# A two-layer block with three token mixers on one core: another order of the projection's chunks, and the preparation of one branch beside the chain of another

## The chip, the cores and the metric

The kernel runs on one core of one Trainium2 chip. The metric is the device time of one execution in microseconds. The engines are called PE (TensorE), DVE (VectorE), ACT (ScalarE), POOL (GpSimd) and SP (SyncE, which here only issues transfers). Each engine works through its own instructions in the order in which they stand in its queue, and semaphores order the engines among each other.

## What is computed

512 tokens of width 1024 pass a first block (attention with pooling, then a mixture of experts) and a second block of two layers. Only the second block's two layers are touched. One such layer, cut to what matters:

```python
h = rms_norm_2(x, norm_g[layer])
cols = split_columns(h @ w_in[layer])          # gate, gdn q/k/v/a/b, mla cq/ckv/kr, rwkv r/k/v/wd/ad
y_gdn = gdn_branch(cols, ...)                  # depthwise conv, silu, gated delta rule, both directions
y_mla = mla_branch(cols, ...)                  # 6 heads of softmax attention over low-rank q and kv
y_rwkv = rwkv7_branch(cols, ...)               # 4 heads, recurrence with its own decay, both directions
mix = jnp.concatenate([y_gdn, y_mla, y_rwkv], axis=-1) * jax.nn.silu(cols['gate'])
x = x + mix @ w_out[layer]

# gdn_branch, per chunk of 64 tokens and head (gated_delta_chunked)
a_mat = beta[..., :, None] * jnp.einsum('nhcid,nhcjd->nhcij', k, k) * d_strict
sol = lax.linalg.triangular_solve(a_mat, rhs, left_side=True, lower=True, unit_diagonal=True)
p_intra = jnp.einsum('nhcid,nhcjd->nhcij', q, k) * d_incl
def step(s, inp):                              # over the 8 chunks
    u = u0_c - jnp.einsum('nhcd,nhde->nhce', w_c, s)
    o = jnp.einsum('nhcd,nhde->nhce', qg_c, s) + jnp.einsum('nhij,nhje->nhie', p_c, u)
    s = ge_c[..., None, None] * s + jnp.einsum('nhcd,nhce->nhde', kd_c, u)
    return s, o
```

## The kernel before

**The projection.** `Project` multiplies the normalized tokens by `w_in` in 27 chunks of 128 output columns. A chunk is 24 matmuls of 128x512 (`columns`, L1221: eight slices of the width, each as the three products hh·wh, hl·wh, hh·wl of a split into two parts). `load` (L1201) fetches a chunk's weights `w` by SP into a ring of two buffers ("pjw"); ACT rounds them to `wh` (L1212), and `wl = w - wh` (L1214) is made by DVE and POOL in turn, two chunks ahead. A ring buffer is free once `wl` is made. The chunk's sum lands in one of three PSUM buffers named "mm". The order before (`self.plan`, L1140 to L1142): first the small columns, then k (three chunks), q (three), v (three), gate 0 to 3, rw 0 to 6, ckv, cq, gate 4 to 7.

**What follows a chunk.** `qkv` (L1276) convolves and activates a chunk on ACT and DVE (four DVE operations on L1289, three more steps to L1299) into `y`, and puts the "take" of the chunk on a list; the take runs when three are pending. `take_q` sums squares on PE (`ssq`). `take_k` transposes to `kt`. `take_v` transposes eight tiles through the single PSUM buffer "tr" and copies each group to `VS` with two operations (L1444), one on ACT and one on DVE. `rw` (L1310) evicts a chunk of the RWKV7 columns with one operation of ACT and two of DVE (L1318, L1319).

**The gated delta branch** (`Gdn`). `keys` (L1500) normalizes `kt` on DVE (L1515), transposes it on PE into `kq`. `squares` (L1549) multiplies k by k for each of four token tiles t (PE, PSUM tile "x2"), ACT copies to `KK`, and DVE multiplies four quarters of 32 partitions into `M` (L1565; 16 operations of 32x384 in a layer). `decays` (L1567) builds `DT` and multiplies it by k·q: 8 DVE operations that read PSUM (L1601), two for each t. `inverse` (L1606) writes `M` to memory and reads it back transposed (`mud`, `au`: L1609, L1612), solves all blocks by 60 DVE operations (`solve`, L1342 and L1344), writes the inverse out and back (`xud`, `XT`: L1618, L1620), transposes on DVE (L1631, L1633), and joins the blocks by 96 small matmuls `x<-XT,AO` and 96 `x<-LT,XT`. `chain` (L1644) then runs eight steps: matmuls `kp`, DVE (L1660, L1662), matmuls `pu`, DVE (L1671), matmuls `kp`, DVE (L1684). An output phase of four rounds follows (L1716, L1729).

**The other branches.** `Rwkv.prepare` (L1802) has per direction a part `scaled` (`lw` L1832, then `BB`, `KR`, `s`, `sq` on L1844 to L1874, with POOL and ACT between), then a triangular solve of its own and `mm<-XT,AO`. `states` (L2021) is its recurrence. `mla` (L2147) is attention in 24 score units (`mm<-kT,qT`, `e`, `mo`), and `Mix` (L2277) gates, transposes (`tr<-mix`) and multiplies by `w_out`.

**What sets the order.** PE's order is written by the program: `weave` and `braid` run several generators ("streams") in turn, and a stream's `yield n` keeps it away for n us of planned PE time. The queues of the other engines are ordered by a scheduler with priorities. In `second` (L2394) the streams were woven so: (1) `first` (gates, triangles, keys, squares, then inverse beside decays) with `project`; (2) `second` (the chain) with `project`; (3) the rest of `project`; (4) `prepare` with `others` (mla, then two thirds of Mix) until prepare ends; (5) `states` with `others`.

## Time and profile before

| | us |
|---|---|
| median of 3 runs | 1932.96 |
| lowest and highest | 1924.71, 1935.54 |
| profiled execution | 1931.57 |
| its span (first to last instruction) | 1929.8 |
| granted clock of PE, mean, as a share of full speed | 0.912 |

The profile is of one execution. Its times count from the start of the span; 1.8 us lie around the span. The second block's first layer stands at about 834 to 1383, the second at about 1383 to 1922. Three kinds of view are used: the waits of an engine (what it waited for, in total, how many times, the longest), the timeline of an engine (each row a run of like instructions, with start and length), and busy times of all engines in a stretch with the granted clock.

### The profile page before, as it was taken

The numbers are of one execution on the slowest core, as the hardware profiler recorded it, in microseconds if no ns is written. First come the engines' busy times: TensorE is split into PE (matmuls) and PEld (weight loads), VectorE is DVE, ScalarE is ACT, GpSimd is POOL, SyncE is SP. The second block draws the span as 40 slices with busy tenths as digits, with TensorE's granted clock in tenths as the row PEclk, the third lists the DMA queues.
The fourth block names the chain that finished last, engine by engine and source line by source line (L and its number), as shares of the span: only waits on it lengthen the run. The fifth ranks groups of instructions, "written<-read, shape, count | busy, mean of one in ns | idle before, by whom it ended". The sixth has DMA issues, their size and how long they took to land.

```text
span 1929.8 us, 34104 instructions
## 1 busy us (share of the span) xinstructions
PE 1675.8 (87%) x14010; PEld 1119.3 (58%) x14010; DVE 1062.8 (55%) x2260; ACT 573.9 (30%) x1134; POOL 548.8 (28%) x559
## 2 busy tenths in 40 slices
PE   5999998999999999968788978768896899888777
PEld 3986584454544444447576746545675677556455
DVE  2435534353434343357796476745867875667437
ACT  3345432212122121154322125331343231154312
POOL 1113111101010101045641154254354612544443
PEclk7899998999999999979898988888898899797888
DMA  9924626999999999532243120143422341301332
GB/s 308 243 94 151 245 66 250 392 393 394 407 402 397 395 406 398 211 112 77 55 148 73 57 75 2 43 138 99 120 74 70 106 110 63 80 1 28 106 118 80
DMA packets 243218, 337.10 MB, mean 175 GB/s; under 512 B 92768, under 2 KB 166160, under 8 KB 226224
## 3 DMA queue, kind: packets, MB, share of 16 engines
q1 hardware_dynamic: 241152, 329.88, 49.6%
q10 hardware_dynamic: 1152, 3.22, 0.5%
q8 instruction: 112, 1.84, 0.4%
q0 software_dynamic: 752, 1.76, 0.3%
q14 instruction: 50, 0.41, 0.1%
HBM read 310.84 MB, written 23.99 MB: 174 GB/s over the span
## 4 chain that ended last, share of the span: by engine, by line
PE 26%; DVE 16%; issue 5%; DMA 4%; POOL 3%; ACT 2%; SPq 0%; DVEq 0%; POOLq 0%; ACTq 0%
PE mm L149 18%; DVE au L1344 2%; PE mm L159 2%; DVE stmp L1342 2%; PE x L149 2%; PE tr L149 1%; PE pu L149 1%; PE kp L149 1%; DVE M L1565 1%; POOL w L2308 1%; DMA w<-in_w_out_dram 1%; DVE wl L1214 1%; PE tr L159 1%; DVE y L1289 1%; PE mo L149 1%
## 5 line engine op out<-in xcount | busy, mean ns | idle before, releaser
L149 PE MATMUL gu<-w,XT 128*64 128x512 f32 x1024 | 225.8, 594 | 0.0
L149 PE MATMUL mm<-hh,wh 128*128 128x512 f32 (+1 forms) x464 | 202.1, 436 | 1.9 <-DVE rw L1319 1.9
L149 PE MATMUL mm<-hl,wh 128*128 128x512 f32 (+1 forms) x464 | 187.3, 404 | 0.0
L149 PE MATMUL mm<-hh,wl 128*128 128x512 f32 (+1 forms) x464 | 187.2, 403 | 0.0
L928 POOL TENSOR_TENSOR yl<-y,yh 128x512 fp32r<-128x512 f32 x30 | 38.1, 1271 | 451.3 <-ACT yh L927 451.3
L149 PEld LDWEIGHTS gu<-w,XT 128*64 128x64 f32 x1024 | 72.1, 137 | 142.7 <-issue 135.6
L938 DVE TENSOR_TENSOR xres<-mm,xres 128x512 f32<-128x512 f32 x128 | 79.2, 681 | 90.6 <-PE mm L149 90.6
L1212 ACT ACTIVATE wh<-w 128x1024 fp32r<-128x1024 f32 (+1 forms) x54 | 57.0, 1055 | 192.8 <-PE mm L149 134.1
L149 PE MATMUL mm<-w,hT 128*64 128x512 f32 x512 | 113.4, 595 | 0.7 <-ACT hT L912 0.7
L149 PEld LDWEIGHTS mm<-hh,wh 128*128 128x128 f32 (+1 forms) x464 | 91.3, 197 | 27.9 <-issue 5.7
L149 PEld LDWEIGHTS mm<-hh,wl 128*128 128x128 f32 (+1 forms) x464 | 90.6, 195 | 21.0
L2236 POOL TENSOR_SCALAR e<-e,rs 128x512 f32<-128x512 f32 x48 | 79.1, 1651 | 80.0 <-DVE rs L2235 58.1
L149 PEld LDWEIGHTS mm<-hl,wh 128*128 128x128 f32 (+1 forms) x464 | 91.6, 197 | 17.5 <-DVE hl L1160 0.2
L1214 POOL TENSOR_TENSOR wl<-w,wh 128x1024 fp32r<-128x1024 f32 (+1 forms) x28 | 68.1, 2431 | 112.3 <-ACT wh L1212 101.7
L149 PE MATMUL mm<-wh,hh 128*128 128x256 f32 x320 | 94.0, 294 | 2.2 <-ACT hh L357 2.2
L149 PE MATMUL mm<-wh,hl 128*128 128x256 f32 x320 | 91.2, 285 | 4.2 <-DVE hl L359 4.0
L149 PE MATMUL mm<-w,mh 128*128 128x512 f32 x256 | 88.6, 429 | 6.7 <-ACT mh L2359 4.1
L149 PE MATMUL mm<-wl,hh 128*128 128x256 f32 x320 | 90.7, 284 | 1.6 <-DVE wl L381 1.6
L149 PEld LDWEIGHTS mm<-w,hT 128*64 128x64 f32 x512 | 35.3, 137 | 66.7 <-issue 61.7
L1342 DVE TENSOR_TENSOR stmp<-au 96x60 f32<-96x60 f32 (+29 forms) x120 | 60.2, 501 | 16.0 <-DMA au<-rmud 8.7
L872 ACT ACTIVATE X<-mm,ws 128x512 f32<-128x512 f32 x32 | 22.0, 689 | 151.9 <-DVE ws L869 128.7
L926 DVE SCALAR_TENSOR_TENSOR y<-mm,ws,g2b 128x512 f32<-128x512 f32 x32 | 24.0, 751 | 78.2 <-PE mm L149 78.2
(580 smaller groups left out, 3678.4 us busy)
## 6 DMA issues: line engine op xcount, KB each, us to landing
w<-in_w_gate_dram SPq DMA_DIRECT2D x64, 1024.0 KB, 13.0
w<-in_w_up_dram SPq DMA_DIRECT2D x64, 1024.0 KB, 13.0
w<-in_w_down_dram SPq DMA_DIRECT2D x64, 1024.0 KB, 9.8
w<-in_w_in_dram SPq DMA_DIRECT2D x52, 512.0 KB, 4.1
w<-in_w_ada_dram SPq DMA_DIRECT2D x24, 1024.0 KB, 8.4
w<-in_w_out_dram SPq DMA_DIRECT2D x16, 512.0 KB, 4.1
w<-in_w_in_dram SPq DMA_DIRECT2D x6, 1024.0 KB, 11.9
w<-in_w_out_dram SPq DMA_DIRECT2D x4, 1024.0 KB, 6.3
```

What stands on the lines that cost most here:

```text
L149: return self.nc.tensor.matmul(out, a, b, **kw)
L159: return self.nc.tensor.transpose(out, a, ident)
L872: nc.scalar.activation(X[:, 512 * i:512 * i + 512], ps, AF.Copy, scale=ws[:, 1:2])
L926: nc.vector.scalar_tensor_tensor(y, py, ws[:, 0:1], net.g2b[:, hs], op0=ALU.mult, op1=ALU.mult)
L928: (nc.vector if last else nc.gpsimd).tensor_tensor(yl[:, hs], y, yh[:, hs].bitcast(F32), op=ALU.subtract)
L938: nc.vector.tensor_tensor(net.xres[:, t, hs], po, net.xres[:, t, hs], op=ALU.add)
L1212: nc.scalar.activation(h[:, :, :m], w[:, :, :m], AF.Copy)
L1214: eng.tensor_tensor(lo[:, :, :m], w[:, :, :m], h[:, :, :m].bitcast(F32), op=ALU.subtract)
L1289: nc.vector.scalar_tensor_tensor(y[:, lo:hi], ps[:, lo + d:hi + d], cw[:, j, m:m + 1], y[:, lo:hi], op0=ALU.mult, op1=ALU.add)
L1342: nc.vector.tensor_tensor(tv, au[:n, :, j + 1:, j:j + 1].to_broadcast(sh), au[:n, :, j:j + 1, 0:j].to_broadcast(sh), op=ALU.mult)
L1344: nc.vector.tensor_tensor(au[:n, :, j + 1:, 0:j], au[:n, :, j + 1:, 0:j], tv, op=ALU.add)
L2236: nc.gpsimd.tensor_scalar(e, e, rs, None, op0=ALU.mult)
```

## The change

The order of the chunks becomes: small columns, k (three), gate 0 to 3, q, v, rw, and the rest as before. The takes are no longer run by `qkv` but by `columns`, when two more chunks have been multiplied after the chunk they belong to. `keys` waits for 19 us of planned PE time rather than 14 before it normalizes. `take_v` copies by ACT only. `M` is multiplied for two token tiles at once: eight DVE operations of 32x768 in a layer rather than 16 of 32x384. The product k·q is copied out of PSUM by ACT into a tile `kr`, and one DVE operation of 128x768 per token tile multiplies it into `DT`. `prepare` is no longer a stream of its own: it runs at the end of `project`, so it is woven with the chain, and `others` begins only when the last chunk is done and the projection's buffers are released.

```diff
--- before.py
+++ after.py
@@ -1138,9 +1138,11 @@
         self.psum = ctx.enter_context(pool(tc, "pjp", 1, "right", PSUM))
         one = lambda n, i, w=128: [(OFF[n] + 128 * i, w)]
         self.plan = [FIRST]
-        self.plan += [one("qkv", m) for m in QKV]
-        self.plan += [one("gate", m) for m in range(4)] + [one("rw", m) for m in range(7)] + [one("ckv", 0), one("cq", 0)] + [one("gate", m) for m in range(4, 8)]
+        self.plan += [one("qkv", m) for m in QKV[:3]] + [one("gate", m) for m in range(4)] + [one("qkv", m) for m in QKV[3:]]
+        self.plan += [one("rw", m) for m in range(7)] + [one("ckv", 0), one("cq", 0)] + [one("gate", m) for m in range(4, 8)]
         self.ahead = []
+
+        self.count, self.pend = 0, []
 
         self.got = KC
 
@@ -1228,6 +1230,9 @@
                 yield 0.3
             yield 0
             mm3(self.net, ps[:m], (h[:, k, :m], lo[:, k, :m]), (self.hh[:, k], self.hl[:, k]), k == 0, k == KC - 1)
+        self.count += 1
+        while self.pend and self.pend[0][0] < self.count:
+            self.pend.pop(0)[1]()
         return ps
 
     def ab(self, ab, mch):
@@ -1273,13 +1278,12 @@
         nc.sync.dma_start(mchd[:, 0::2], mch[:, 0::2])
         nc.sync.dma_start(mchd[0:96, 1], mch[0:96, 1])
 
-    def qkv(self, g):
+    def qkv(self, g, ms):
 
 
         net, nc, tmp = self.net, self.net.nc, self.tmp
         cw = net.smalls.cw[:, self.l]
-        pend = []
-        for m in QKV:
+        for m in ms:
             ps = yield from self.columns()
             y = tmp.tile([128, S], F32, name="y", bufs=4)
             nc.scalar.activation(y, ps, AF.Copy, scale=cw[:, 2, m:m + 1])
@@ -1297,15 +1301,11 @@
                 nc.scalar.activation(c8(y), z, AF.Square)
             else:
                 nc.vector.scalar_tensor_tensor(y, th, 1.0, y, op0=ALU.add, op1=ALU.mult)
-            pend.append((m, partial((g.take_q, g.take_k, g.take_v)[m // 3], self, m % 3, y)))
-            if len(pend) > 2:
-                i0, f = pend.pop(0)
-                f()
-                g.have.add(i0)
-        for i0, f in pend:
-            yield 5
-            f()
-            g.have.add(i0)
+            self.pend.append((self.count + 1, partial(self.take, g, m, y)))
+
+    def take(self, g, m, y):
+        (g.take_q, g.take_k, g.take_v)[m // 3](self, m % 3, y)
+        g.have.add(m)
 
     def rw(self, rw):
 
@@ -1441,7 +1441,7 @@
             pv = ps.rearrange("p (t a c) -> p t a c", t=NT, a=2)
             for h in range(2):
                 dst = self.VS[half(h)].rearrange("p (s z) (a m) c -> p z s a m c", z=2, m=3)[:, h if d == 0 else 1 - h, :, :, m]
-                (nc.vector.tensor_copy if h else nc.scalar.copy)(dst, pv[half(h)])
+                nc.scalar.copy(dst, pv[half(h)])
 
     def gates(self):
 
@@ -1509,7 +1509,7 @@
             nc.gpsimd.tensor_tensor(sq, kv, kv, op=ALU.mult)
             nc.vector.tensor_reduce(ss[:, t], sq, AX.X, ALU.add)
         r = net.rstd(tmp, ss.rearrange("p t h -> p (t h)"), [128, 24], 1, 1e-6, "rk").rearrange("p (t h) -> p t h", t=NT)
-        yield 14
+        yield 19
         for t in range(NT):
             kv = kt[:, t].rearrange("p (h d) -> p h d", d=64)
             nc.vector.tensor_tensor(kv, kv, r[:, t, :, None].to_broadcast([128, 6, 64]), op=ALU.mult)
@@ -1560,9 +1560,11 @@
                         net.matmul(ps[half(c), par, hp * 64:hp * 64 + 64], kq[half(par), hp, 2 * t + c, 0:64],
                                          kq[half(par), hp, 2 * t + c, 0:64], start=True, stop=True)
             nc.scalar.activation(KK[:, us].rearrange("p (a h) c -> p a (h c)", a=2), ps[:, :, :192], AF.Copy)
-            for b in range(4):
-                q, o = quarter(b), 32 * (b % 2)
-                nc.vector.tensor_tensor(M[q, :, us], KK[q, None, us, o:o + 32].to_broadcast([32, 2, 6, 32]), M[q, :, us], op=ALU.mult)
+            if t % 2:
+                us = slice(6 * t - 6, 6 * t + 6)
+                for b in range(4):
+                    q, o = quarter(b), 32 * (b % 2)
+                    nc.vector.tensor_tensor(M[q, :, us], KK[q, None, us, o:o + 32].to_broadcast([32, 2, 12, 32]), M[q, :, us], op=ALU.mult)
 
     def decays(self, ptd):
 
@@ -1596,9 +1598,9 @@
                     for c in range(2):
                         net.matmul(ps[half(c), par, hp * 64:hp * 64 + 64], kq[half(par), hp, 2 * t + c, 0:64],
                                          kq[half(par), hp, 2 * t + c, 64:128], start=True, stop=True)
-            for d in range(2):
-                dv = DT[:, d, us].rearrange("p (a h) c -> p a h c", a=2)
-                nc.vector.tensor_tensor(dv, dv, ps[:, :, :192].rearrange("p a (h c) -> p a h c", h=3), op=ALU.mult)
+            kr = tmp.tile([128, 6, 64], F32, name="rh")
+            nc.scalar.activation(kr.rearrange("p (a h) c -> p a (h c)", a=2), ps[:, :, :192], AF.Copy)
+            nc.vector.tensor_tensor(DT[:, :, us], DT[:, :, us], kr[:, None].to_broadcast([128, 2, 6, 64]), op=ALU.mult)
         nc.sync.dma_start(ptd, DT)
         self.decayed = True
         self.ends()
@@ -2431,12 +2433,15 @@
             third = Rwkv(net, a, l, rw, lk)
 
             def project():
-                yield from pj.qkv(g)
+                yield from pj.qkv(g, QKV[:3])
                 third.weights()
                 yield from pj.gate(gated, range(4))
+                yield from pj.qkv(g, QKV[3:])
                 yield from pj.rw(rw)
                 yield from net.braid(third.first(pj), pj.latents(mch, mchd), pj.gate(gated, range(4, 8)))
                 pj_stack.close()
+                g.have.add("all")
+                yield from third.prepare(rmud, rxud)
 
             def first():
                 yield from g.gates()
@@ -2453,6 +2458,8 @@
 
             def others():
                 nonlocal mix
+                while "all" not in g.have:
+                    yield 0.5
                 yield from mla(net, a, l, mchd, mixt, tabd)
                 mix = Mix(net, a, l, mixd, mixt, gated, xd, xstack)
                 for k in (0, 3):
@@ -2462,12 +2469,10 @@
                     yield 8
                     yield from mix.rows(3)
 
-            project, first, second, others, prepare, states = (
-                project(), first(), second(), others(), third.prepare(rmud, rxud), third.states())
+            project, first, second, others, states = project(), first(), second(), others(), third.states()
             net.weave(first, project, until=first)
             net.weave(second, project, until=second)
-            net.weave(project)
-            net.weave(prepare, others, until=prepare)
+            net.weave(project, others, until=project)
             net.weave(states, others, until=states)
             net.weave(others)
             mix.done = -1
```

How the change moves instructions. First the queue of SP in the first layer, where M is written for the solve. `w` is the load of a chunk's weights, which waits for a free ring buffer; `mud` is M in memory, `au` its transposed copy, `gated` a gate chunk on its way out. Before:

```order
L1049 DMA w<-in_w_in_dram 128x8x128 x10
L1609 DMA mud_7551<-M 128x1536
L1612 DMA au<-mud_7551 48x64x32 x2
L1049 DMA w<-in_w_in_dram 128x8x128
L1329 DMA gated_7548<-gt 128x512 x2
```

After:

```order
L1329 DMA gated_7548<-gt 128x512 x2
L1049 DMA w<-in_w_in_dram 128x8x128 x4
L1611 DMA mud_7551<-M 128x1536
L1049 DMA w<-in_w_in_dram 128x8x128
L1614 DMA au<-mud_7551 48x64x32 x2
L1049 DMA w<-in_w_in_dram 128x8x128 x3
```

The write of M and its reading back stood together; now one load of weights stands between them, and the loads ahead of them are for later chunks (15 and 16 of the plan) than before.

Next the queue of DVE behind the solve in the first layer: `XT` is the solved inverse, `rw<-mm` evicts an RWKV7 chunk from PSUM. Before:

```order
L1318 SCALAR_TENSOR_TENSOR rw<-mm,smalls,rw 128x511
L1319 SCALAR_TENSOR_TENSOR rw<-mm,smalls,rw 128x511
L1780 TENSOR_SCALAR kx<-rw,smalls 128x512
L1631 STREAM_TRANSPOSE LT<-XT 32x24x32 x4
L1214 TENSOR_TENSOR wl<-w,wh 128x1024
```

After:

```order
L1216 TENSOR_TENSOR wl<-w,wh 128x1024
L1318 SCALAR_TENSOR_TENSOR rw<-mm,smalls,rw 128x511
L1319 SCALAR_TENSOR_TENSOR rw<-mm,smalls,rw 128x511
L1633 STREAM_TRANSPOSE LT<-XT 32x24x32 x4
L1635 STREAM_TRANSPOSE XT<-LT 32x768
L1318 SCALAR_TENSOR_TENSOR rw<-mm,smalls,rw 128x511
L1635 STREAM_TRANSPOSE XT<-LT 32x768
L1319 SCALAR_TENSOR_TENSOR rw<-mm,smalls,rw 128x511
```

The pair of rw evictions among the transposes is that of chunk rw 5, after it follows rw 6; before, rw 4 stood at that place (behind the rows shown), and rw 5 and 6 followed. `tr<-cst,rw` on PE transposes chunks rw 4 and 5 together.

On PE, `tr<-cst,rw` and `tr<-cst,th` (transposes of the RWKV7 chunks and sums over heads) stand around the products with XT. Before:

```order
L149 MATMUL mm<-hh,wl 128x512
L149 MATMUL x_9022<-XT,AO 32x32 x96
L159 MATMUL tr<-cst,rw 128x128 x4
L149 MATMUL mm<-hh,wh 128x512
L149 MATMUL mm<-hl,wh 128x512
```

After:

```order
L149 MATMUL tr<-cst,th 128x2 x4
L149 MATMUL x_9111<-XT,AO 32x32 x96
L149 MATMUL tr<-cst,rkk 64x128 x8
L149 MATMUL x_9219<-LT,XT 32x32 x96
L149 MATMUL tr<-cst,rkk 64x128 x8
```

Two groups of `tr<-cst,rw`, two of `tr<-cst,th` and 36 chunk matmuls between them, which followed `x<-XT,AO` before, now stand ahead of it.

Last, the queue of DVE in the last steps of the chain (SA, rhs and VS are the chain's own; lw, rks, BB and s belong to `prepare`). Before:

```order
L1684 TENSOR_TENSOR SA<-SA,kp 128x384
L1660 TENSOR_TENSOR rhs<-kp,GS 128x384
L1662 TENSOR_TENSOR rhs<-VS,rhs 128x384
L1328 SCALAR_TENSOR_TENSOR gt<-gt,mm 128x512
L1671 TENSOR_TENSOR VS<-pu,FS 128x384
```

After:

```order
L1673 TENSOR_TENSOR VS<-pu,FS 128x384
L1834 TENSOR_TENSOR lw<-mm,w_7716 128x256
L1973 TENSOR_SCALAR rks<-cst,smalls 128x2 x2
L1834 TENSOR_TENSOR lw<-mm,w_7716 128x256 x2
L1686 TENSOR_TENSOR SA<-SA,kp 128x384
L1834 TENSOR_TENSOR lw<-mm,w_7716 128x256
L1662 TENSOR_TENSOR rhs<-kp,GS 128x384
L1664 TENSOR_TENSOR rhs<-VS,rhs 128x384
L1846 SCALAR_TENSOR_TENSOR BB<-s_9886,rw 128x512
L1847 TENSOR_SCALAR s_9886<-s_9886,smalls 128x512
L1673 TENSOR_TENSOR VS<-pu,FS 128x384
L1848 TENSOR_TENSOR BB<-s_9886,rw 128x512
```

Both directions' `scaled` parts of `prepare` now stand between the operations of the last chain steps and of the output phase. On PE, `mla` begins after them, `mm<-XT,AO` of the RWKV7 branch comes after 18 of mla's 24 score units (before: after all 24), and the first `tr<-mix` comes after five of the recurrence's steps (before: after two).

## Rows read from the trace of the kernel before

**Rows 1.** The page: busy time of each engine, share of the span, instructions.

```profile
PE 1675.8 (87%) x14010; PEld 1119.3 (58%) x14010; DVE 1062.8 (55%) x2260; ACT 573.9 (30%) x1134; POOL 548.8 (28%) x559
```

**Rows 2.** Waits of PE, 862 to 1383: engine, waiting, releaser: total us, times, longest.

```profile
PE tr L159 <- DVE VS L1444: 12.0, 3, 7.0
PE x L149 <- DVE DT L1601: 6.2, 1, 6.2
PE tr L159 <- DVE kt L1515: 5.0, 1, 5.0
```

**Rows 3.** Busy time by stretch; columns are named in its first line.

```profile
core 0: us, PE busy (x) PEld busy (x) DVE busy (x) ACT busy (x) POOL busy (x), PEclk, DMA share, GB/s
1041.00:1110.00 69.00, 62.26 (x760) 48.52 (x752) 34.21 (x78) 9.41 (x14) 12.78 (x17) 0.88 0.15 48
1121.00:1176.00 55.00, 44.64 (x337) 22.87 (x337) 39.73 (x68) 20.46 (x40) 22.36 (x27) 0.78 0.21 53
1176.00:1278.00 102.00, 78.23 (x1157) 55.74 (x1155) 67.38 (x175) 44.29 (x104) 50.95 (x39) 0.92 0.16 40
1661.00:1715.00 54.00, 44.74 (x335) 22.10 (x335) 40.18 (x67) 20.38 (x40) 22.79 (x27) 0.78 0.23 54
1715.00:1817.00 102.00, 85.30 (x1166) 60.05 (x1169) 67.49 (x177) 44.45 (x104) 52.01 (x40) 0.85 0.16 41
```

**Rows 4.** Timeline of VectorE: start, us, engine, line, operation, count [idle before].

```profile
922.89 2.23 DVE L1565 TENSOR_TENSOR M<-KK,M 32x384 f32<-32x384 f32 x4
928.67 4.38 DVE L1565 TENSOR_TENSOR M<-KK,M 32x384 f32<-32x384 f32 x4
937.77 3.34 DVE L1565 TENSOR_TENSOR M<-KK,M 32x384 f32<-32x384 f32 x4
951.57 0.25 DVE L1342 TENSOR_TENSOR stmp<-au 96x60 f32<-96x60 f32 x1 [2.24 <-DMA au<-mud]
```

**Rows 5.** Timeline of GpSimd, one row of the same time.

```profile
928.14 2.81 POOL L1214 TENSOR_TENSOR wl<-w,wh 128x1024 fp32r<-128x1024 f32 x1 [6.78 <-ACT wh L1212]
```

**Rows 6.** Timeline of SyncE's queue, the write of M.

```profile
941.14 0.33 SPq L1609 DMA_DIRECT2D mud<-M  x1
```

**Rows 7.** Waits of SyncE's queue, 880 to 1120; L1049 loads projection weights.

```profile
SPq L1049 <- POOL wl L1214: 52.7, 8, 15.6
```

**Rows 8.** Timeline of VectorE behind the solve.

```profile
1017.60 3.94 DVE L1631 STREAM_TRANSPOSE LT<-XT 32x768 f32<-32x768 f32 x4 [3.83 <-DMA XT<-xud]
1025.49 0.75 DVE L1319 SCALAR_TENSOR_TENSOR rw<-mm,smalls,rw 128x511 f32<-128x511 f32 x1
```

**Rows 9.** Timeline of PE where it reaches XT.

```profile
1027.38 0.39 PE L149 MATMUL mm<-hl,wh 128*128 128x512 f32 x1
1027.61 0.39 PE L149 MATMUL mm<-hh,wl 128*128 128x512 f32 x1
1027.92 1.47 PE L149 MATMUL x<-XT,AO 32*32 32x32 f32 x151
```

**Rows 10.** Timeline of VectorE, preparation of the RWKV7 branch.

```profile
1121.66 0.42 DVE L1832 TENSOR_TENSOR lw<-mm,w 128x256 f32<-128x256 f32 x1
1159.00 0.68 DVE L1874 TENSOR_TENSOR s<-BB,cl 128x512 f32<-128x512 f32 x1
1259.86 0.71 DVE L2004 STREAM_TRANSPOSE XT<-LT 32x512 f32<-32x512 f32 x1
```

**Rows 11.** Timeline of PE: attention, RWKV7 states, first product of the mix.

```profile
1263.99 1.09 PE L149 MATMUL mo<-t,vt 128*64 128x128 f32 x16
1267.77 1.09 PE L149 MATMUL mo<-t,vt 128*64 128x128 f32 x16
1271.87 1.29 PE L149 MATMUL mm<-XT,AO 32*32 32x32 f32 x128
1286.38 1.09 PE L149 MATMUL mo<-t,vt 128*64 128x128 f32 x14 [0.38 <-ACT t L2244]
1303.57 0.90 PE L159 MATMUL tr<-cst,mix 128*128 128x128 f32 x3 [9.15 <-DMA mix<-mixd]
```

## The prediction

> **What bounds the kernel now.** I read the busy times first: PE works 87% of the span [rows 1], so what can be won is PE's idle time and its half-speed stretches in the two layers that the change touches. I then read PE's waits in the first layer. Three of them are aimed at: transposes of v wait 12.0 us for the copy of VS, the longest 7.0; normalized keys cost 5.0; the k.q products wait 6.2 for DT [rows 2]. The second layer repeats the pattern, so each step is worked out in the first. Last I read the stretches. In the chain (1041 to 1110) PE is busy 62.26 of 69 us and DVE 34.21. Behind the chain, in the RWKV7 preparation beside the attention (1121 to 1278), PE has 122.9 us of work in 157, a granted clock of 0.78 in its first 55 us, and DVE 107.1 [rows 3]. So the chain is nearly PE's own time, with DVE half free, and the stage behind it is a relay between engines: 34.1 us of idle PE there is the largest reserve of the layer.
>
> **From k to M.** The wait for keys (5.0) and the longest wait for VS (7.0) go [rows 2]: gate chunks, which owe nothing to the keys, fill the one, and the other's transposes move behind the squares. Against these 12 us PE does 30 more chunk matmuls ahead of the last square. Their starts are 0.23 us apart [rows 9], so 6.8 us. Of the rest I give back 1, since weights now come in shorter succession. The last M is ready 4.5 us earlier, at 936.6 instead of 941.1 [rows 6].
>
> M's own operations: four of 32x384 took 2.23 us when DVE was undisturbed and 4.38 while POOL made wl [rows 4, 5]. A paired one has 768 elements. The nearest bounds are one old operation (0.56) and two old ones with POOL busy (2.2); I take 0.95, near twice the smaller less one start. On the path stand four operations in either kernel, the last token tile's before, the last two tiles' now: 3.8 instead of 3.34 [rows 4], no gain, -1 to +5. The Trainium skill (SBUF — State Buffer, Terms) says that VectorE and GpSimd hold their shared port pair exclusively for a whole instruction and that the loser fully blocks. By that a paired operation behind a wl of POOL would start up to 2.81 us later once [rows 5], and the sum would be 3 us worse a layer; the row shows four operations that cost 2.15 us more together under one such wl, spread or not, and I keep the smaller effect.
>
> **To the solve.** The load of weights now ahead of M's write waits until an earlier wl is made, and on DVE that wl stands behind some eleven operations of the convolutions, which are like the 0.75 of [rows 8], about 8 us behind the last M. M's write therefore goes out at 945 rather than 941.14 [rows 6]; the bounds of this wait are 0 and the 15.6 that the longest such wait on SP took [rows 7]. What queues behind it on SP is the reading of au, and DVE's solve waits for that. From the write to the first solve operation it took 10.4 us [rows 4, 6], and from there to XT transposed 73.9 [rows 4, 8]; the work of DVE in between is about the same (one more chunk's evictions, four k.q operations of 768 for eight of 384). XT is ready at 945 + 10.4 + 73.9 = 1029, about 4 us later.
>
> The k.q edit costs four ACT copies and saves about half a us of DVE; ACT is busy 30% of the span [rows 1]. Its wait of 6.2 [rows 2] may go, but nothing earlier than XT comes out of that: PE gets further ahead with chunks and then waits for XT. V's copies by ACT alone are the same case. I count both at nothing; if ACT were late, at 1 to 3.
>
> **PE ahead of XT.** Before, the product with XT started at 1027.92, 2.4 us behind XT, among chunk matmuls [rows 8, 9]. Now both transposes of rw 4 and 5 stand ahead of it, and the eviction of rw 5 stands behind the first XT transposes on DVE. PE can only begin 36 chunk matmuls and 16 transposes when XT is there already: 36 x 0.23 + some 3 = 11 us at full clock, up to 20 at half, behind an idle PE. XT on PE: about 1041, 13 later. In the second layer rw 5 is evicted during the solve, so there it is about 4.
>
> **The chain with prepare.** Before, from XT to the end of the output phase: 1027.9 to about 1121, 93 us. The 36 matmuls already done leave the steps; they are half hidden beside DVE, so -4. Prepare's scaled parts enter: 26 operations, those between the first two of [rows 10] that are not the chain's or the attention's. They hold some 18 of DVE's 39.73 us in that stretch [rows 3]: 11 in the last steps, 7 in the output phase. DVE has half its time free there [rows 3], but they stand between the links in DVE's queue, so I charge 8 of 18. The chain ends 13 + 4 = 17 later, at 1138.
>
> **What is then already done.** Before, the first such operation ran at 1121.66 and the second direction's at 1159.7; from there to the RWKV7 inverse (1260.6) it took 101 us [rows 10]. Those 101 remain: 1138 + 100 = 1238, 22 earlier. PE reached that inverse at 1271.87, 11 us late, with six attention units ahead that now stand behind it: start to start, two units take 3.78 us [rows 11], so 11.3. PE reaches it at 1240, 32 earlier. From there to the last attention product were 15.6 us, plus the six units 11.3, plus 3 for sharing PE with the recurrence: 1270 instead of 1287.5 [rows 11]. The mix waits for that through memory, as before 16.1 us: 1286 instead of 1303.57, **-17 us in the first layer**. The recurrence steps that move ahead of it I leave uncounted.
>
> The second layer by the same steps, XT only 4 late: the chain ends 8 late, the preparation is 31 early, the mix 25. There the stage has 156 us with 130.0 of PE's work [rows 3], 8 less idle than the first, which I take off: **-17**.
>
> Sum: -34 on the profiled 1931.57, 1.4 under the median: **1898 us**. By itself this forecast spans 1880 to 1918: 10 us for each layer's XT (0 to 20 at half clock), 5 for the hidden share of the 18.
>
> **Rivals.** *All cover holds*: M's write is not delayed (-8 a layer) and rw 5 is evicted in time (-10 in the first): -34 - 26 = 1872. For it: DVE is busy only 55% [rows 1] and a queue's order shows no time. Against: both orders are in the queues in both layers.
>
> *The solve starts late*: the weights' load waits as long as the longest did, 15.6 [rows 7] rather than 8.4, and the second load, between M's write and its reading, waits another 7, in both layers: -34 + 28 = -6, 1926. It decides once both waits add 12 in each layer. PE's stalls were then only cover for DVE's solve, and the wait moves to XT. For it: the 73.9 us from solve to XT are DVE's own, and nothing in the change shortens them.
>
> *Slower: the relay moves into the chain whole.* The 38 us that the scaled parts took (1121.66 to 1159.7 [rows 10]) were mostly waits between PE, ACT, POOL and DVE. In DVE's queue each operation that waits holds the chain's next link. I charged 8; from 25 in each layer on nothing is won, at 34 (nearly all) the time is 1898 + 2 x 26 = 1950. Against: rows of lw and BB have their inputs ready while PE's chain runs.
>
> **How the numbers follow.** Forecast 0.52, all cover 0.17, late solve 0.18, slower 0.13. Within 0.5% means 1922 to 1942, about what a measurement can tell from no change. Faster: the first two and a little of the third, 0.70; same: 0.17; slower: 0.13. For 8 in 10 the range reaches into both outer cases: 1868 to 1940.
>
> **What would show it.** In the changed profile: no wait for kt, and VS waits under 4 (right: first step). M's write within 4 us of 945, the first solve operation near 955, `x<-XT,AO` near 1041 in the first layer and behind chunk matmuls that start after XT. Chain steps of 7 to 9 us in the last three, an output phase of about 15; a step of 15 would be the slower case. `mm<-XT,AO` of RWKV7 near 1240 and the first `tr<-mix` near 1286; if it stands at 1303 with the waits above gone, the late solve has eaten them. The prediction is wrong if the time lies over 1922 with M's write on time.

## The result, and the profile of the changed kernel

The changed kernel takes 1906.67 us (median of 6 runs, 1902.15 to 1911.97), the kernel before 1928.72 beside it (6 runs). The ratio is 0.9883 with a 95% interval of 0.9864 to 0.9903: 22 us less, where 34 were forecast. The profiled execution took 1903.25, of which 1901.5 are its span, 28.3 less than before's 1929.8; it lies 3.4 under the kernel's median, so the profile shows a little more than the medians. One execution of the kernel that is called prepare only below, 1951.57 us at a clock of 0.901, belongs to a slow state and is left out of its median and ratio.

The page (busy time, share of the span, instructions), which answers [rows 1]:

```profile
PE 1653.5 (87%) x14010; PEld 1100.7 (58%) x14010; DVE 1046.3 (55%) x2224; ACT 583.7 (31%) x1154; POOL 558.4 (29%) x559
```

PE does the same 14010 matmuls in 22.3 us less busy time, at a mean granted clock of 0.930 rather than 0.912: of the 28.3 us of span only 6 are idle time that was filled. The waits of PE in the first layer (840 to 1400: total us, times, longest) answer [rows 2]:

```profile
PE mm L159 <- POOL e L2238: 10.2, 2, 7.4
PE tr L159 <- DMA mix<-mixd: 9.7, 1, 9.7
PE tr L159 <- ACT VS L1444: 6.8, 3, 2.6
...
PE x L149 <- ACT rh L1602: 5.8, 1, 5.8
...
PE tr L159 <- ACT rw L1317: 4.2, 1, 4.2
```

The wait for `kt` is gone and that for VS is down from 12.0 to 6.8, where under 4 was forecast. DT's wait has only changed its name: 6.2 for DVE then, 5.8 for ACT's copy of k.q now. The 4.2 for the eviction of an RWKV7 chunk are new, and the wait for POOL's `e` in the attention has grown from 3.0 to 10.2.

To see where time went I split each layer at five marks of the timelines: XT transposed on DVE, first `x<-XT,AO` on PE, last `pu` of the output phase, last `mo` of the attention, first `tr<-mix`. What the table calls the layer's start is the first transpose of the gates on PE (`tr<-go`), some 45 us into the layer. Lengths in us, first layer / second layer:

| | before | after | forecast, first layer |
|---|---|---|---|
| layer's start to XT ready | 146.5 / 146.8 | 139.5 / 144.1 | +4 |
| PE behind XT | 2.5 / 2.5 | 14.5 / 3.1 | +9 |
| product with XT to end of output phase | 92.9 / 86.0 | 91.0 / 90.9 | +4 |
| end of output phase to last `mo` | 166.7 / 164.0 | 151.2 / 142.5 | -34 |
| last `mo` to `tr<-mix` | 16.1 / 14.8 | 15.9 / 14.6 | 0 |
| `tr<-mix` to the layer's last `xres` | 80.4 / 83.3 | 85.0 / 82.3 | 0 |

The first layer is 8 us shorter, the second 20; 17 were forecast for each. These lengths, and all those below, are of one execution of each kernel. The steps' own rows follow. First the timeline of DVE, then that of SP (start, us, engine, line, operation), which answer [rows 4, 6]:

```profile
922.20 3.84 DVE L1567 TENSOR_TENSOR M<-KK,M 32x768 f32<-32x768 f32 x4 [1.07 <-ACT KK L1562]
...
926.27 1.23 DVE L1216 TENSOR_TENSOR wl<-w,wh 128x1024 fp32r<-128x1024 f32 x1
...
928.08 1.90 DVE L1567 TENSOR_TENSOR M<-KK,M 32x768 f32<-32x768 f32 x2
...
930.79 2.84 DVE L1567 TENSOR_TENSOR M<-KK,M 32x768 f32<-32x768 f32 x2
...
946.47 0.26 DVE L1342 TENSOR_TENSOR stmp<-au 96x60 f32<-96x60 f32 x1 [2.81 <-DMA au<-mud]
```

```profile
927.53 0.54 SPq L1049 DMA_DIRECT2D w<-in_w_in_dram  x1
933.66 0.33 SPq L1611 DMA_DIRECT2D mud<-M  x1
936.60 0.54 SPq L1049 DMA_DIRECT2D w<-in_w_in_dram  x1
```

M's write goes out as soon as M is there. The load ahead of it has left SP at 928.1: the `wl` that freed its buffer ran on DVE at 926.3, ahead of the last M. Then the timeline of PE where it reaches XT, as [rows 9]:

```profile
1018.32 0.87 PE L159 MATMUL tr<-cst,rw 128*128 128x128 f32 x3 [4.20 <-ACT rw L1317]
...
1031.92 1.27 PE L149 MATMUL x<-XT,AO 32*32 32x32 f32 x127
```

XT was ready at 1017.4. PE was then in its wait for the eviction, and a stretch of chunk matmuls and transposes stands between that and the product.

### The profile page after: what moved, and what is told of

The parts are those of the page before. It is cut to its first block, busy times and chain, and to the rows that moved or that the text cites. A ratio compares the mean times of both kernels' runs of the same rounds, so it can differ in the third digit from the quotient of the medians.

```text
span 1901.5 us, 34119 instructions
## 1 busy us (share of the span) xinstructions
PE 1653.5 (87%) x14010; PEld 1100.7 (58%) x14010; DVE 1046.3 (55%) x2224; ACT 583.7 (31%) x1154; POOL 558.4 (29%) x559
## 4 chain that ended last, share of the span: by engine, by line
PE 25%; DVE 17%; DMA 5%; issue 4%; POOL 3%; ACT 2%; SPq 1%; DVEq 0%; POOLq 0%; ACTq 0%
PE mm L149 17%; DVE stmp L1342 2%; DVE au L1344 2%; PE mm L159 2%; PE tr L149 1%; PE x L149 1%; PE pu L149 1%; PE kp L149 1%; DMA w<-in_w_out_dram 1%; DMA au<-mud 1%; DVE nm L2233 1%; DVE y L1293 1%; PE mo L149 1%; DMA gate<-gated 1%; POOL w L2310 1%
## 5 line engine op out<-in xcount | busy, mean ns | idle before, releaser
L149 PE MATMUL mm<-w,mh 128*128 128x512 f32 x256 | 92.9, 442 | 22.8 <-POOL w L2310 10.0
L149 PEld LDWEIGHTS mm<-w,mh 128*128 128x128 f32 x256 | 50.1, 206 | 41.1 <-POOL w L2310 12.5
L1342 DVE TENSOR_TENSOR stmp<-au 96x60 f32<-96x60 f32 (+29 forms) x120 | 64.5, 537 | 14.3 <-DMA au<-rmud 6.5
```

What stands on the lines that cost most here:

```text
L149: return self.nc.tensor.matmul(out, a, b, **kw)
L1342: nc.vector.tensor_tensor(tv, au[:n, :, j + 1:, j:j + 1].to_broadcast(sh), au[:n, :, j:j + 1, 0:j].to_broadcast(sh), op=ALU.mult)
```

## The experiments

The change has three parts that can be done apart: the **order** of chunks, the small **edits** (v by ACT, M in pairs, k.q by ACT) and **prepare** beside the chain. The expectations' theory A is the prediction's own: the gain comes from prepare. The other letters are other theories, as told there. The takes that run two chunks later belong to the change, but to none of the three parts: they stand in every kernel of the table but prepare only, and were not tested by themselves.

| kernel | median us | ratio to before, 95% interval |
|---|---|---|
| order only | 1932.60 | 1.0006, 0.9990 to 1.0023 |
| edits only | 1921.31 | 0.9949, 0.9930 to 0.9967 |
| prepare only | 1928.06 | 1.0020, 0.9997 to 1.0043 |
| order and edits | 1901.93 | 0.9872, 0.9840 to 0.9904 |
| edits and prepare | 1923.97 | 0.9989, 0.9969 to 1.0008 |
| order and prepare | 1915.46 | 0.9935, 0.9913 to 0.9957 |
| all three (after) | 1906.67 | 0.9883, 0.9864 to 0.9903 |

**Prepare, undone and alone.** From after, and the same edit the other way round on before:

```diff
                 pj_stack.close()
-                g.have.add("all")
-                yield from third.prepare(rmud, rxud)
...
-            net.weave(project, others, until=project)
+            net.weave(project)
+            net.weave(prepare, others, until=prepare)
```

> The changed kernel with one part undone: the preparation is again a stream of its own behind the chain, woven with the attention. Chunk order, copies by ScalarE and the paired M stay. Theory A (the gain is the preparation's relay hidden beside the chain; what the new order saves in front of the inverse is lost in PE's order ahead of XT): 1920 to 1932 us, within 0.5% of the kernel before; output phase of the first layer ends within 5 us of 1121, first lw at its end and not at 1091, first transpose of the mix near 1303. Theory B (the gain is the stalls in front, 12 to 18 us a layer): 1903 to 1912, like the changed kernel.

> The kernel before with one part of the change alone: the preparation runs at the end of the projection's stream beside the chain, and the attention waits for the last chunk. Theory A: 1903 to 1914 us, nearly all of the gain; the RWKV7 inverse 20 to 35 us earlier in each layer against the layer's start, the stalls on keys (5.0), VS (12.0) and DT (6.2) unchanged. Theory B: 1920 to 1932.

Measured 1901.93 and 1928.06. Without prepare beside the chain the new kernel is as fast as with it, and the part alone does not make the old one faster: theory A, by which nearly all of the gain comes from there, falls. The part alone is the weaker test, for in the old order little of prepare gets into the chain. Busy times of the stretch from the product with XT to the end of the output phase, first layer, before and then prepare only (columns as in [rows 3]):

```profile
1027.92:1120.82 92.90, 81.78 (x1556) 65.85 (x1555) 47.22 (x104) 13.03 (x20) 20.36 (x27) 0.89 0.18 55
```

```profile
1027.47:1123.05 95.58, 85.84 (x1566) 67.58 (x1565) 48.67 (x108) 15.08 (x25) 21.16 (x30) 0.89 0.17 54
```

Ten matmuls of prepare have entered it, and of DVE's operations its four `lw` and two more; in after 52 matmuls and 22 operations of DVE enter, 16 of these 22 being `BB`, `KR`, `s` and `sq`. In the new order the part is tested. Busy times of the same stretch, first layer, prepare a stream of its own and then after:

```profile
1031.79:1112.53 80.74, 69.17 (x1496) 55.94 (x1495) 41.73 (x100) 8.26 (x12) 18.24 (x26) 0.87 0.15 47
```

```profile
1031.92:1122.90 90.98, 78.53 (x1548) 61.13 (x1548) 54.97 (x122) 15.85 (x26) 23.53 (x33) 0.92 0.13 43
```

The stretch grows by 10.2 us, and PE's work in it by 9.4: its idle time is 11.6 and 12.5. The second layer has the same: 10.5 longer, 8.3 more of PE's work. Little or nothing of what was moved in is hidden here. Whoever waits for the chain is put off by as much, and that is the attention. SP's timeline, the attention's first load, in the one and in the other:

```profile
1112.61 0.37 SPq L2163 DMA_DIRECT2D mch<-mchd  x1
```

```profile
1122.99 0.37 SPq L2163 DMA_DIRECT2D mch<-mchd  x1
```

In both it goes out 0.1 us behind the chain's last matmul (in before too, 1120.90 behind 1120.8). In after SP has waited for the output phase by then:

```profile
SPq L2163 <- DVE rhs L1718: 16.3, 1, 16.3
```

And the attention ends last: measured from the chain's end, the RWKV7 inverse (`mm<-XT,AO` on PE) comes at 120 and 106 rather than 143 and 142, but the last `mo` only at 151 and 143 rather than 156 and 157. So 4 and 15 us are won behind the chain for 10 lost in it.

This price is not the same in every kernel. With order and prepare (all three edits undone, below) against the order alone the move is worth 0.7%, 17 us, and the intervals lie apart; with edits and prepare against the edits alone it costs 0.4%. The chain and the stage behind it, first layer, the order alone and then order and prepare:

```profile
1039.34:1121.52 82.18, 70.46 (x1496) 57.04 (x1495) 41.87 (x100) 8.25 (x12) 18.21 (x26) 0.85 0.15 47
1121.52:1282.17 160.65, 131.41 (x1605) 84.77 (x1607) 110.10 (x247) 67.54 (x149) 75.21 (x69) 0.87 0.17 44
```

```profile
1034.96:1127.43 92.47, 79.79 (x1548) 62.58 (x1548) 54.77 (x122) 15.77 (x26) 23.67 (x33) 0.91 0.13 42
1127.43:1269.94 142.51, 122.76 (x1745) 77.28 (x1748) 99.64 (x234) 60.43 (x135) 72.64 (x68) 0.89 0.19 50
```

The chain grows by 10 and 11 us in the two layers, as it did above, but the stage behind it is shorter by 18 and 17 rather than by 4 and 15. What the move costs is steady in the new order; what it gives back hangs on how the stage behind the chain comes out.

**Order undone, order alone, edits alone.** In all three the takes still run two chunks later. The order alone is prepare and the edits undone, the edits alone are prepare and the order undone.

```diff
-        self.plan += [one("qkv", m) for m in QKV[:3]] + [one("gate", m) for m in range(4)] + [one("qkv", m) for m in QKV[3:]]
+        self.plan += [one("qkv", m) for m in QKV]
...
-        yield 19
+        yield 14
```

> The changed kernel with the chunk order of before (k, q, v, then gate 0 to 3) and the wait of 14 ahead of the keys; the preparation beside the chain and the copies by ScalarE stay. Theory A: 1903 to 1914 us, no difference from the changed kernel that can be measured, although waits on keys and VS of 10 us or more come back in each layer. Theory B: 1918 to 1930.

> The kernel before with the new chunk order, the deferred takes and the wait of 19 ahead of the keys, and nothing else: v leaves PSUM by both engines, M and k.q as before, the preparation a stream of its own. Theory C (the order fills the stalls on keys and v, and the copies by ScalarE are what lets the takes of v run without a stall; both are needed): 1910 to 1920 us. Theory D (the order alone does it, the edits of single operations are hidden): 1898 to 1908, like the kernel that has order and edits (1902).

> The kernel before with the edits of single operations alone: v's copies all on ScalarE, M for two token tiles at once, k.q out of PSUM by ScalarE, takes counted in the chunk loop; chunk order and preparation as before. Theory C: 1916 to 1924 us. Theory D: 1924 to 1932, no difference. With the preparation beside the chain as well it was 1924.

Measured 1923.97, 1932.60 and 1921.31. The first is as theory B and the last as theory C had it; the order alone is slower than either theory allowed. With prepare on its own the order by itself is worth nothing, the edits 0.5%, both 1.3%; beside prepare, however, the order is worth 0.8%, without the edits. PE's waits in the first layer of the order alone:

```profile
PE tr L159 <- DVE VS L1444: 15.7, 3, 8.6
```

The order removes the wait for `kt`, but brings the takes of v to a busier DVE (43.4 of 46.0 us from 954 to 1000, where before it was 22.4 of 30.6 from 923.5 to 954.1), so the copies by both engines cost 15.7 rather than the 12.0 of [rows 2]; with order and edits it is 6.3. That is one reason why order and edits go together, and not the whole: with order and prepare the wait is 15.6, and that kernel is 17 us faster than the order alone.

Where the gain of order and edits lies can be read from the marks. Their two layers are 32 us shorter than before's. 12 of these come ahead of XT. The chain is 18 shorter, but PE comes to XT 18 later, since the matmuls that left the chain now stand there. 18 lie in the stage behind the chain, where nothing was edited, and 2 behind that.

**The edits one by one**, each undone in after, and all three undone:

```diff
-                nc.scalar.copy(dst, pv[half(h)])
+                (nc.vector.tensor_copy if h else nc.scalar.copy)(dst, pv[half(h)])
```

```diff
-            if t % 2:
-                us = slice(6 * t - 6, 6 * t + 6)
...
+            for b in range(4):
```

```diff
-            kr = tmp.tile([128, 6, 64], F32, name="rh")
...
+            for d in range(2):
```

> The changed kernel with v's copies again half on VectorE. Order and edits gave -1.3% together, the order alone nothing and the edits alone -0.5%, so one of the edits lets the order work. If it is v's copies (PE's waits on VS were 6.3 with ScalarE alone and 15.7 with both engines in the new order): those waits at 13 or more in each layer, XT 3 to 6 us later, 1916 to 1926 us. If the edits only add up: 1909 to 1914.

> The changed kernel with M multiplied for each token tile by itself (16 operations of 32x384 a layer). If v's copies are what counts: 1905 to 1911, M written 1 to 3 us later. If the pairing is what counts, because M's operations meet POOL's wl and stand in front of the convolutions: 1914 to 1924.

> The changed kernel with k.q again multiplied out of PSUM by VectorE, 8 operations of 128x384 a layer. If v's copies are what counts: 1904 to 1911, PE's wait in front of the second k.q product 2 to 7 us as now. If it is this edit, because VectorE's solve holds the operations that PE waits for: 1914 to 1924.

> The changed kernel with all three edits undone: new order and preparation beside the chain alone. With the other seven combinations this completes the table of three parts. If order and edits work only together and the preparation's place is worth nothing: 1924 to 1936 us. If the preparation beside the chain makes up for them: 1910 to 1920.

| undone in after | median us | ratio to before, 95% interval |
|---|---|---|
| v by ACT | 1916.17 | 0.9944, 0.9927 to 0.9962 |
| M in pairs | 1932.72 | 1.0028, 1.0012 to 1.0044 |
| k.q by ACT | 1908.18 | 0.9904, 0.9885 to 0.9923 |
| all three | 1915.46 | 0.9935, 0.9913 to 0.9957 |

V by DVE again costs 0.6%, with VS waits of 17.4 and 17.7 us in the two layers, as the first reading had it; k.q costs nothing that can be measured. M unpaired costs 26 us, more than either reading allowed, and yet unpairing it along with the others costs 9. No price of M's operations can do that. All three undone is the order and prepare of above: of the two readings, the one in which prepare makes up for the edits came true. In the first layer the kernel with single M is as long as after (497.0 and 497.1 us from the layer's start to its last `xres`); the 28 us are all in the second (505.8 and 477.5): 9 in PE's wait for XT, 16 behind the chain, 3 in the dense part. Behind the chain the queue of DVE differs. Its timeline in the second layer of after, `nm` being the row maximum of the attention and `stmp` the solve of the RWKV7 branch, which waits for a transfer:

```profile
1717.44 0.68 DVE L2233 TENSOR_REDUCE nm<-mm 128x1 f32<-128x512 f32 x1
...
1720.20 0.20 DVE L1342 TENSOR_TENSOR stmp<-au 128x30 f32<-128x30 f32 x1 [2.09 <-DMA au<-rmud]
```

The same with single M:

```profile
1727.45 0.20 DVE L1342 TENSOR_TENSOR stmp<-au 128x30 f32<-128x30 f32 x1 [4.11 <-DMA au<-rmud]
...
1732.27 0.68 DVE L2231 TENSOR_REDUCE nm<-mm 128x1 f32<-128x512 f32 x1
```

The first maximum now stands behind the solve's first operations, and the attention waits with them for the transfer. The longest of PE's waits there becomes that for the attention's `e`:

```profile
PE mm L159 <- POOL e L2236: 8.0, 1, 8.0
```

The stretch from the chain's end to the last `mo`, after and then single M:

```profile
1655.10:1797.60 142.50, 120.92 (x1746) 76.92 (x1744) 99.51 (x234) 60.58 (x135) 72.15 (x68) 0.90 0.19 50
```

```profile
1663.10:1821.50 158.40, 128.20 (x1741) 81.33 (x1740) 100.15 (x234) 60.87 (x135) 70.11 (x68) 0.84 0.17 45
```

Over the ten layers of after and of the kernels with single M, half of v, k.q undone or all edits undone, the stretch is 142.3 to 142.5 us in the three where `nm` is ahead, and 143.4 to 158.5 in the other seven, of which the first layer of after is one (151.2). Where it stands behind, something else decides too, by the width of that range. Nor does the order decide by itself: with prepare only, and in the last kernel of this section (after with XT ahead), five or six maxima stand ahead of the solve and the stretch is 158.2 to 165.5 us. So that the flip costs the 16 us is a reading of the queues and not shown. The edit of M is far from that place: the scheduler that orders DVE's queue came to another order there. What it weighed was not tested.

A like flip stands in ACT's queue in kernels with prepare on its own. Its timeline in the first layer of before: three attention exponentials `e` stand ahead of the scan's (`ci`, `s`), for which PE waits 2.67 us (second fence, PE's timeline).

```profile
1180.65 0.69 ACT L2234 ACTIVATE e<-mm,nm 128x512 f32<-128x512 f32 x1 [1.21 <-POOL e L2236]
...
1181.33 0.59 ACT L1859 ACTIVATE ci<-mm 128x512 f32<-128x512 f32 x1
1181.81 0.60 ACT L1860 ACTIVATE s<-mm 128x512 f32<-128x512 f32 x1
```

```profile
1182.45 2.06 PE L149 MATMUL mm<-cst,lw 128*128 128x128 f32 x8 [2.67 <-ACT s L1860]
```

With order and edits two stand ahead, without a wait of PE:

```profile
1169.41 0.69 ACT L2236 ACTIVATE e<-mm,nm 128x512 f32<-128x512 f32 x1
...
1170.38 0.60 ACT L1861 ACTIVATE ci<-mm 128x512 f32<-128x512 f32 x1 [0.19 <-PE mm L149]
```

In the ten layers of five such kernels (before, order only, edits only, order and edits, and order and edits with XT ahead, below) the wait goes with a stretch of 160.6 to 166.7 us and its absence with 155.6 to 157.6, for the same matmuls. That is a coincidence in ten of ten, not an experiment on the queue. If it is the cause, it is the larger part of what order and edits win, for in their kernel both layers are without the wait and in before both have it.

**PE ahead of XT.** The RWKV7 chunks whose eviction holds PE first (chunks 4, 5, 6, 0, 1, 2, 3):

```diff
...
-        for m in range(7):
+        for m in (4, 5, 6, 0, 1, 2, 3):
```

> The changed kernel with the RWKV7 chunks in the order 4, 5, 6, 0, 1, 2, 3, so that the two chunks that PE transposes ahead of the product with XT are evicted during the solve. If PE's transposes behind the late eviction of chunk 5 cost what the trace shows (4.2 us of waiting in the first layer and matmuls at a lower clock behind it): the product with XT in the first layer at 1024 to 1028 instead of 1031.9, 1898 to 1904 us in all. If the matmuls moved ahead are only missing later in the chain: 1904 to 1910, no difference.

Measured 1910.76, 0.9910 (0.9879 to 0.9941): no gain over after. `x<-XT,AO` still starts at 1032.1 in the first layer, and PE's waits there show another one in the eviction's place:

```profile
PE tr L159 <- ACT vt L1775: 5.3, 1, 5.3
```

Then the product itself was moved ahead of those transposes, in the kernel with order and edits and in after. The number is the planned time after which `inverse` joins the blocks:

```diff
-        yield 26
+        yield 15
         yield from off_diagonal(net, lambda: self.pa.tile([128, 2, 512], F32, name="x2", bufs=1), self.AO, XP, LT, T, 24, fac)
```

> Order and edits with the preparation as a stream of its own (1902 us), and the planned wait in front of the product with XT cut from 26 to 15 us: on PE it then stands ahead of the transposes of rw 4 and 5 and of the 36 chunk matmuls behind them, as it did in the kernel before. If the path from XT through the chain to the attention sets the layer's end: the product 8 to 10 us earlier in each layer (11.6 behind XT now), 1882 to 1890 us in all. If PE's work between the solve and the attention sets it, the matmuls come back in the chain, whose length grows by what is won: 1898 to 1906.

> The changed kernel with the same cut of the planned wait (26 to 15). Same two readings: 1890 to 1898 us (14.5 and 3.1 behind XT now, so some 10 in the first layer and little in the second), or no difference from the changed kernel, 1903 to 1911.

Measured 1895.67, 0.9828 (0.9801 to 0.9855), and 1903.30, 0.9851 (0.9824 to 0.9878). The first is the fastest kernel of the study: order, edits, prepare on its own, XT ahead. It lies between the two readings, the second in that of no difference. PE's timeline in the first layer of the fastest:

```profile
1011.33 0.24 PE L149 MATMUL x<-XT,AO 32*32 32x32 f32 x2
1014.75 0.25 PE L149 MATMUL x<-XT,AO 32*32 32x32 f32 x4 [3.17 <-DVE XT L1635]
1016.53 2.23 PE L149 MATMUL x<-XT,AO 32*32 32x32 f32 x148 [1.54 <-DVE XT L1635]
```

PE now waits for XT, 4.7 us in all, rather than XT for PE. The bulk of the product starts 15 us earlier, but the chunk matmuls that stood ahead of it come back between the links: the stretch from the product's first matmul to the output phase's end grows from 80.7 to 91.2. From the layer's start to that end 6 us are won in each layer, of 11.8 and 11.4 by which PE had been late; in the second layer the stage behind the chain, with the wait for the scan's exponentials, takes 8 back. The ratio falls by 0.0044, some 8 us, and its interval still touches that of order and edits, though not that of after. In after itself the ratio fell by 0.0032, some 6 us, within the intervals.

## Why the prediction was nearly right in time and wrong in its reasons

The time lay in the range and on the forecast's side, and that is luck. The forecast promised 34 us where 22 came, and it had all of them from moving prepare beside the chain; up to the product with XT it counted 13 us lost in the first layer. The kernel without that move is as fast as the one with it, so the gain comes from order and edits. The steps erred in both directions.

**From k to M: right in direction.** M was ready at 933.6, 7.5 us earlier, where 4.5 were worked out (its own terms, 12 less 6.8 less 1, give 4.2); 1 us of it was there at the layer's start. A paired operation takes 0.96 us (3.84 for four), 0.95 was taken, but the four on the path took 4.74 and not 3.8: the last two were held up beside POOL, as told at the end.

**M's write: wrong.** It was to wait until 945 for a load's buffer. The ring's `wl` was set some eleven operations behind the last M; it was done ahead of it. The order of a queue was read rightly, but which `wl` frees which buffer was not followed. So the solve began at 946.5 instead of 955, and XT was ready at 1017.4 instead of 1029. DVE's timeline, the last operation on it:

```profile
1016.42 0.97 DVE L1635 STREAM_TRANSPOSE XT<-LT 32x768 f32<-32x768 f32 x1
```

**PE ahead of XT: right.** 12 us behind XT were worked out, 14.5 measured; about 4 in the second layer, 3.1 measured. The small wait of the second layer is after's own: in the kernels with one edit undone, or all, it is 11.8 to 15.4.

**The chain: two terms mis-sized that cancelled.** The 36 chunk matmuls that leave it were charged -4, as half hidden beside DVE. With prepare outside, the stretch is 80.7 rather than 92.9: they and the transposes with them were worth 12 (80.4 rather than 86.0, so 6, in the second layer). The 18 us of DVE work that enter were charged +8; measured are +10.2. The step did not count the 9.4 us of PE's work that come with them, and the growth of the stretch is about that. Net -2 instead of +4 in the first layer, +5 in the second, and the chain's end came at 1122.9 instead of 1138.

**What is then already done: the step that failed.** First, front matter and prediction say that both directions' scaled parts moved into the chain. They are the two halves of the columns of one direction; the second direction's begin at 1134.5, behind the chain. The sum used the right length all the same, from the end of the first to the inverse: 101 was to remain, and 112.6 remain in the first layer, from 1121.8 to 1234.4. DVE's timeline, as [rows 10]:

```profile
1121.15 0.68 DVE L1876 TENSOR_TENSOR sq<-BB,cl 128x512 f32<-128x512 f32 x1
...
1134.54 0.74 DVE L1834 TENSOR_TENSOR lw<-mm,w 128x256 f32<-128x256 f32 x2
...
1233.69 0.71 DVE L2006 STREAM_TRANSPOSE XT<-LT 32x512 f32<-32x512 f32 x1
```

Second, the step took the RWKV7 inverse as what ends the stage and the attention as its companion. The inverse did come 28.6 us earlier on PE (1243.3, where 1240 was worked out), but from a chain that ended 15 us earlier than worked out, so its own part took longer. But what ends the stage is the attention, whose loads leave only when the chain has ended, so the 10 us by which prepare lengthens the chain put it off by as much. The stage shrank by 15 and 22 instead of 34 and some 25 (33 less the 8 taken off). Of that, 11 and 7 are there without prepare's move: compare 155.6 and 157.0 with order and edits to 166.7 and 164.0 before. So the term of the sum that stood for the whole gain, prepare's time already done, was sized at -34 for the first layer; the move itself shortened the stage by 4 there and by 15 in the second, for 10 more in the chain of each. The first `tr<-mix` came at 1290.0, near the 1286 worked out, because the early XT and the late attention cancelled.

**V and k.q at nothing: wrong and right.** V's copy by ACT is worth 0.6% in the new order; k.q's price is not to be told from nothing.

**Rivals.** That all cover holds was right for M's write and wrong for PE's way to XT. A late solve did not come. The relay's move into the chain cost 10, far from the 25 at which nothing would be won; yet nothing was won by it in after, because what it gave back was smaller than reckoned too.

What stays open: why the stage behind the chain comes out at 142 to 158 us in after and the kernels with its edits undone, and at 156 to 167 where prepare is on its own; why it runs with different granted clocks (0.82 to 0.89 where prepare is on its own), and what tips the scheduler. One and the same kernel's time goes with the clock too: prepare only took 1918.79 us at a mean of 0.923 and 1939.44 at 0.906.

## What to carry to other kernels

Before work is moved into a stretch because an engine there is half free, count the work it brings for the engine that is not, and ask who starts when that stretch ends. Test parts of a change both alone and undone: here the order was worth nothing alone and 0.8% beside either of the others, and prepare's place between 0.7% and -0.4%, by what stood beside it. Before a part is called tested alone, look in the trace whether its work went where the edit was to bring it. Where a scheduler orders queues, compare these at the busiest place of the program, however far from the edit, before an edit's own operations get the credit.

## What the runs showed of the hardware

Of the four M operations of before that took 4.38 us [rows 4], one carried the whole delay. All the M operations in 927 to 933, min, median and max in ns:

```profile
L1565 DVE TENSOR_TENSOR M<-KK,M x6: 548/552/2692, 926.9 to 932.5; 32x384 f32<-32x384 f32 x6
```

It began 0.53 us behind POOL's wl, at 928.67, and ended 0.4 behind wl's end at 930.95 [rows 5]: a DVE operation with two inputs in SBUF that met this POOL operation stood still until that was over. In the second layer it is the same: 2.60 us, ending 0.4 behind a wl of POOL. The prediction had called this spread or not, and weighed it against the Trainium skill (SBUF — State Buffer, Terms), which says that the loser of the shared ports fully blocks: the row bears the page out. In after POOL's next wl began only at 934.2, behind the last M, but the shorter operations of POOL on `DT` and `AO` (930.7 to 934.1) met the last two paired ones, which took 1.58 and 1.25 us rather than 0.95.

The stage behind the chain has the same matmuls in before and in the kernel with order and edits, and ran at different clocks. Busy times of that stretch, first and second layer of before, then of the other (columns as in [rows 3]):

```profile
1120.80:1287.50 166.70, 132.01 (x1606) 85.86 (x1608) 109.75 (x247) 67.59 (x149) 75.26 (x69) 0.86 0.17 43
1660.80:1824.80 164.00, 137.62 (x1605) 88.28 (x1607) 110.16 (x247) 67.67 (x149) 75.77 (x69) 0.82 0.18 43
```

```profile
1112.53:1268.10 155.57, 128.65 (x1604) 81.58 (x1604) 109.42 (x247) 67.61 (x149) 75.24 (x69) 0.89 0.18 46
1641.80:1798.90 157.10, 128.21 (x1606) 82.27 (x1608) 110.93 (x247) 67.27 (x149) 75.83 (x69) 0.89 0.18 45
```

PE's busy time is 3.4 and 9.4 us longer at the lower clock. That is a third of the 11.1 us by which the first layer's stage is longer, and more than the 6.9 of the second's. The lower clock goes in the main with the wait for the scan's exponentials shown above (0.82 to 0.87 in the six layers with it, 0.86 to 0.89 in the four without); that the wait brings it about was not shown.
